# Queries, keys and all gates as units of seven products, one root for all norms, heads between the products

## The chip, the cores and the metric

The kernel runs on one core of a Trainium2 chip. The core has a matrix engine (TensorE, "PE" in the profile; its weight loads are "PEld"), a vector engine (VectorE, DVE), a scalar engine (ScalarE, ACT), GpSimd (POOL) and SyncE (SP), which issues every DMA of this kernel. Each engine runs its own instructions in order, and semaphores order the engines among one another. The metric is the device time of one execution in microseconds (us); for a kernel the median of its runs is given. Everything is computed in float32.

## The reference

One decoder block over 1024 tokens of width 1024. What matters here is the first half: one input projection of the normalised input, whose columns are cut into attention queries, keys and values (12 heads of 128), retention q and k (4 heads of 256), retention v and its gate (2048 each) and two merge gates (1024 each).

```python
xn = rmsnorm(x, norm1_g[l])
qa, ka, va, qr, kr, vr, gr, gate_a, gate_b = [xn @ wl[:, bounds[i]:bounds[i + 1]] ...]
qa = rmsnorm(qa.reshape(B, S, ATT_HEADS, ATT_HEAD_DIM), q_norm_g[l])
ka = rmsnorm(ka.reshape(B, S, ATT_HEADS, ATT_HEAD_DIM), k_norm_g[l])
...
s = einsum(q, k) * (Dh ** -0.5) + bias          # ALiBi, causal window, dilated by 1, 4 or 16
p = exp(s - m);  den = sum(p);  o = (p @ v) / den;  lse = m + log(den)
o_a = sum over the three groups of softmax(lse) * o
o_r = head_groupnorm(retention(qr, kr, vr)) * silu(gr)
y = sigmoid(gate_a) * (o_a @ w_proj_a) + sigmoid(gate_b) * (o_r @ w_proj_b)
```

Then follow an output projection with a residual and a squared-ReLU MLP with another.

## The kernel before, in words

**Products.** A float32 operand is split into a high and a low part, `xh` and `xl` (line 318, `split`: ScalarE rounds the high part, L319, VectorE subtracts, L320). A product is the sum of three matmuls, high by high, high by low, low by high (`Pipe.group`, L218 to L230; the matmul is L223). TensorE's order is written out by hand: `Pipe.step` (L232) issues one product, and small tasks that were put down with `pipe.at(lag, fn)` are issued between the terms of the step `lag` steps later. The instructions of the other engines are ordered by a planner from its own estimate of times, the earlier in the program the more urgent; at run time every queue keeps that fixed order.

**Weights.** `Weights` (L38 to L204) loads pieces of weight from DRAM into raw buffers, splits them into six pairs of buffers, and lets the next piece in as a product frees its own. `add` takes a plain piece, `add_units` (L95) those of a unit of seven products.

**Units of seven products.** A block of 256 output columns by 1024 tokens is made of seven half-size products in place of eight (N1 to N7, `product`, L369 to L405, order in `strassen_order`, L257). A unit is 7 x 12 = 84 matmuls of 512 columns. Four of the seven operands are sums and differences of quarters of the input and lie ready in on-chip memory; the weight side's sums are made by VectorE (L121). As products end, ScalarE copies some PSUM banks (L388, L393, L396) and `result` gets the four quarters of the output.

**Order of the first half.**

1. Norm of the input, tile by tile (L548), turned by TensorE (L415) into the operands `X`.
2. Twelve heads (L564 to L679). For each of eight tiles of 128 tokens one step of 24 matmuls with 384 columns makes q, k and v together (L645). ScalarE squares q and k (L650), VectorE and GpSimd make the root of two sums (`rsqrt`, L330 to L333: GpSimd's power of -0.5), VectorE scales (L654), TensorE turns q and k (L660) into `qT` and `kT`. `attend` (L575) makes, for each of eight blocks, three tasks: scores (L584, with the maximum on VectorE at L587 and Exp on ScalarE at L591), the turn of the weights (L597, copied by VectorE at L599) and the product with the values (L604, copied by ScalarE at L606). They lie between the matmuls of later steps. Their PSUM tiles come from the pool `ms` of three. A head's result of 130 columns goes to `acc_d` in one to two DMAs (L612 to L618). Dilated heads send their values through DRAM (`v_d`) to gather them by stride.
3. Three gate blocks as plain products (L695 to L732), while the last head's attention ends; VectorE makes the sums and differences of the input (`differences`, L708).
4. 21 units (L767): five gates, eight of retention q and k, eight of the retention gate. `gate_out` (L687) takes a Sigmoid (L689); the retention gate takes another (L746); results go to DRAM.
5. Retention (L806 on), with the last head slot's mixing of the three groups (`load_heads`, `combine`: L432 to L478), and then the projections and the MLP, which the change leaves alone.

Of the kernel before, what the change touches and what calls it, by code (L numbers as in the profile page):

```python
# [10 lines left out]
F = mybir.dt.float32  # L11
# [6 lines left out]
P = 128  # L18
# [19 lines left out]
class Weights:  # L38
# [56 lines left out]
    def add_units(self, tag, srcs):  # L95
# [28 lines left out]
        for j in range(-1, len(srcs)):  # L124
            if j + 1 < len(srcs):
                r = base + 2 * (j + 1)
                piece((tag, j + 1, "A"), self.A[(j + 1) % 2], r + 1, both)
            if j >= 0:
                r = base + 2 * j
                piece((tag, j, "D"), (self.D, j % 2), r, slice(0, 512), lambda r=r: sums(r))  # L130
                piece((tag, j, "B"), self.B[j % 2], r + 1, both, lambda r=r: self.used.add(r + 1))
                piece((tag, j, "C"), self.C, r, both, lambda r=r: self.used.add(r))
        m = len(srcs)
# [136 lines left out]
def hybrid_block(ctx: ExitStack, tc: tile.TileContext, a: dict, out: bass.AP):  # L270
# [9 lines left out]
    big = pool(ctx, "big", 4)  # L280
# [14 lines left out]
    v_d = dram.tile([HEADS, S, DH], F, name="v_d")  # L295
# [9 lines left out]
    XS = {(j, i): slot_of(big) for i in range(2) for j in range(2)}  # L305
# [22 lines left out]
    const.tile([P, 224], F, name="rest")  # L328
# [89 lines left out]
    def dilated(g, b, src, dst):  # L418

        if g == 0:  # L420
            return src, dst[:, b * P:(b + 1) * P]
        r = 4 if g == 1 else 8
        src = src.rearrange("p (i r) -> p r i", r=r)
        if g == 1:
            nb, j = divmod(b, 4)
            return src, dst.rearrange("p (r i) -> p r i", r=r)[:, :, nb * P + 32 * j:nb * P + 32 * j + 32]
        return src, dst.rearrange("p (r i) -> p r i", r=r)[:, :, 16 * b:16 * b + 16]
# [4 lines left out]
    def load_heads(s, i, p2b):  # L432
        at = p2b.tile([P, 4, 3, DH + 2], F, name="at", bufs=1)
        rows = acc_d[512 * i:512 * i + 512].rearrange("(t p) (g s) e -> s p t g e", p=P, s=SLOTS)
        for t in range(4):
            tc.keep_in_program_order(nc.sync.dma_start(at[:, t], rows[s, :, t]))
        return at

    def combine(s, i, p2b, at):


        st = {}
        return [lambda: weigh(p2b, at, st), *(lambda t=t: mix(t, at, st) for t in range(4)),
                lambda: turn_mixed(s, i, p2b, st)]

    def weigh(p2b, at, st):
        w = st["w"] = p2b.tile([P, 6, 4], F, name="w")
        st["o"] = p2b.tile([P, 4, DH], F, name="oa")
# [23 lines left out]
    def turn_mixed(s, i, p2b, st):  # L472
        pt = tr.tile([P, 4, P], F, name="tr")
        for t in range(4):
            nc.tensor.transpose(pt[:, t, :], st["o"][:, t, :], ident)
        ot = p2b.tile([P, 512], F, name="oaT")
        nc.scalar.activation(ot, pt.rearrange("p t q -> p (t q)"), AF.Copy)
        nc.sync.dma_start(oa_d[s, :, 512 * i:512 * i + 512], ot)  # L478
# [11 lines left out]
    attn = ExitStack()  # L490
    p3 = pool(attn, "p3", 2, "right")
    p2 = pool(attn, "p2", 2, "right")
    cpa = pool(attn, "cpa", 1, "right")
    with ExitStack() as ph:
        cp = pool(ph, "cp", 1)
        first = ExitStack()
        px = pool(first, "px", 2)
        cmb = None

        g1 = cp.tile([P, D], F, name="g1")  # L500
        gq = cpa.tile([P, HEADS], F, name="gq")
        gk = cpa.tile([P, HEADS], F, name="gk")
        dist = cp.tile([P, 2, 2 * P], F, name="dist")
        row = px.tile([P, D], F, name="xn", bufs=3)
        ones = cp.tile([1, P], F, name="ones")
        xts = {}

        def load_x(t):
            xts[t] = px.tile([P, D], F, name="xt", bufs=3)
            nc.sync.dma_start(xts[t], a["x"][t * P:(t + 1) * P, :])  # L510

        xts[0] = px.tile([P, D], F, name="xt", bufs=3)
        for cs in halves():
            nc.sync.dma_start(xts[0][:, cs], a["x"][0:P, cs])
        nc.sync.dma_start(row[0:1, :], a["norm1_g"][None, :])
        nc.sync.dma_start(ident, a["c_ident"])
        W.load()
        W.load()
        load_x(1)
        W.load()  # L520
        ss = px.tile([P, 4], F, name="ss")
        xn = px.tile([P, D], F, name="xn", bufs=3)
        lo, hi = halves()
        gp = [mm.tile([P, 512], F, name="mm") for _ in range(2)]
        with tc.manual_schedule(engines={mybir.EngineType.DVE, mybir.EngineType.Activation}):
            nc.vector.memset(ones, 1.0)
            nc.scalar.activation(ss[:, 3:4], half[:, 0:1], AF.Square)
            for cs, pm in zip(halves(), gp):
                nc.tensor.matmul(pm, ones, row[0:1, cs], start=True, stop=True)
            nc.scalar.activation(xn[:, lo], xts[0][:, lo], AF.Square, accum_out=ss[:, 0:1])  # L530
            nc.vector.tensor_tensor_reduce(xn[:, hi], xts[0][:, hi], xts[0][:, hi], op0=OP.mult, op1=OP.add,
                                           scale=1.0, scalar=0.0, accum_out=ss[:, 1:2])
            nc.vector.tensor_tensor(ss[:, 0:1], ss[:, 0:1], ss[:, 1:2], op=OP.add)
            rsqrt(ss[:, 2:3], ss[:, 0:1], 1.0 / D)
            nc.vector.tensor_copy(g1[:, lo], gp[0])
            nc.vector.scalar_tensor_tensor(xn[:, lo], xts[0][:, lo], ss[:, 2:3], g1[:, lo], op0=OP.mult, op1=OP.mult)
            W.pump(1)
            nc.scalar.activation(g1[:, hi], gp[1], AF.Copy)
            nc.vector.scalar_tensor_tensor(xn[:, hi], xts[0][:, hi], ss[:, 2:3], g1[:, hi], op0=OP.mult, op1=OP.mult)
            put_transposed(xn, 0, 0)  # L540
            W.pump(1)
            put_transposed(xn, 0, 1)
            W.pump(1)
        load_x(2)
        load_x(3)
        W.pump(1)

        def norm1(t):  # L548
            if t not in xts:
                load_x(t)  # L550
            ss = px.tile([P, 4], F, name="ss")
            xn = px.tile([P, D], F, name="xn", bufs=3)
            nc.scalar.activation(xn, xts[t], AF.Square, accum_out=ss[:, 0:1])
            rsqrt(ss[:, 1:2], ss[:, 0:1], 1.0 / D)
            nc.vector.scalar_tensor_tensor(xn, xts[t], ss[:, 1:2], g1, op0=OP.mult, op1=OP.mult)
            pipe.at(t - 1 - pipe.slot, *[lambda q=q: put_transposed(xn, t, q) for q in range(2)])

        norm1(1)
        pipe.at(0, lambda: W.pump())
        nc.sync.dma_start(gq, a["q_norm_g"])  # L560
        nc.sync.dma_start(gk, a["k_norm_g"])
        nc.sync.dma_start(dist, a["c_dist"])

        for head, (slot, g) in enumerate(heads):  # L564
            h = g * SLOTS + slot
            slope = 2.0 ** (-8.0 * (h + 1) / HEADS)
            us = W.take(4)
            bias = p2.tile([P, 2 * P], F, name="bias")
            qT = p2.tile([P, S], F, name="qT")
            kT = p2.tile([P, S], F, name="kT")  # L570
            V = p2.tile([P, NT, DH], F, name="V")
            Vd = p2.tile([P, NT, DH], F, name="Vd") if g > 0 else V
            acc = p2.tile([P, NT, DH + 2], F, name="acc")

            def attend(g, h, b, bias, qT, kT, V, acc):  # L575

                nk = 2 if has_prev(g, b) else 1
                n = nk * P
                k0 = (b + 1 - nk) * P
                st = {}  # L580

                def scores():
                    sp = ms.tile([P, 512], F, name="ms")
                    nc.tensor.matmul(sp[:, :n], qT[:, b * P:(b + 1) * P], kT[:, k0:k0 + n], start=True, stop=True)  # L584
                    s = p3.tile([P, 2 * P], F, name="s")
                    mx = p3.tile([P, 1], F, name="mx")
                    nc.vector.tensor_tensor_reduce(s[:, :n], sp[:, :n], bias[:, 2 * P - n:], op0=OP.add, op1=OP.max,  # L587
                                                   scale=1.0, scalar=-3.0e38, accum_out=mx)
                    nc.vector.tensor_scalar(acc[:, b, DH:DH + 1], mx, -1.0, None, op0=OP.mult)
# [773 lines left out]
```

## Time and profile before

| what | value |
|---|---|
| time, median of 3 runs | 2261.97 us (2261.68 to 2267.01) |
| span of the profiled execution | 2267.2 us |
| its busy time on TensorE | 2233.0 us (98%) |
| VectorE / ScalarE / GpSimd busy | 57% / 45% / 15% |
| heads, 10.64 to 521.84 | 511.20 us |
| plain gates and the last head's end, to 595.36 | 73.52 us |
| 21 units, to 995.42 | 400.06 us |
| the rest, to the end | 1271.78 us |
| granted TensorE clock | 0.998 |

The profile is a trace of one execution; its span of 2267.2 us is that of the slowest of the three timed runs. Rows of instructions read: line, engine, operation, output <- inputs, shapes, count, then busy time, mean duration in ns of one, and the idle time of the engine before them. A row of one line's view has the duration as minimum/median/maximum, and the first and last start. A row of a timeline begins with start and duration in us. A row of stretches has the length, then the busy time and the instructions of each engine, the clock, the share of the DMA engines and GB/s. Matmuls overlap on TensorE, so that the mean duration of one (389 ns for 512 columns) is longer than the distance between two starts.

### The profile page before, as it was taken

The numbers are of one execution on the slowest core, as the hardware profiler recorded it, in microseconds if no ns is written. First come the engines' busy times: TensorE is split into PE (matmuls) and PEld (weight loads), VectorE is DVE, ScalarE is ACT, GpSimd is POOL, SyncE is SP. The second block draws the span as 40 slices with busy tenths as digits, with TensorE's granted clock in tenths as the row PEclk, the third lists the DMA queues.
The fourth block names the chain that finished last, engine by engine and source line by source line (L and its number), as shares of the span: only waits on it lengthen the run. The fifth ranks groups of instructions, "written<-read, shape, count | busy, mean of one in ns | idle before, by whom it ended". The sixth has DMA issues, their size and how long they took to land. (4 is left out here: it accounts for less than half of the span.)

```text
span 2267.2 us, 30458 instructions
## 1 busy us (share of the span) xinstructions
PE 2233.0 (98%) x10868; PEld 1912.0 (84%) x10868; DVE 1285.7 (57%) x2468; ACT 1014.0 (45%) x2294; POOL 344.3 (15%) x372
## 2 busy tenths in 40 slices
PE   8999999999999999999999999999999999899999
PEld 7999999998888888888888878888788888788777
DVE  6444545455544445558676753253855556687874
ACT  5444434345433333345555633112555545654542
POOL 1111111110000000000000000000000000587873
PEclk9999999999999999999999999999999999999999
DMA  4313232323233333363433385554345556645432
GB/s 148 98 52 105 65 91 85 94 85 99 82 109 106 110 109 111 113 186 117 122 117 97 121 267 183 155 184 153 107 127 151 151 152 199 218 153 179 169 129 102
DMA packets 227146, 294.85 MB, mean 130 GB/s; under 512 B 14129, under 2 KB 157873, under 8 KB 226994
## 3 DMA queue, kind: packets, MB, share of 16 engines
q1 hardware_dynamic: 226994, 292.91, 41.1%
q8 instruction: 85, 1.39, 0.3%
q14 instruction: 67, 0.55, 0.1%
HBM read 200.48 MB, written 92.37 MB: 129 GB/s over the span
## 5 line engine op out<-in xcount | busy, mean ns | idle before, releaser
L320 DVE TENSOR_TENSOR wl<-raw,wh 128x1024 fp32r<-128x1024 f32 (+2 forms) x274 | 300.4, 1099 | 398.0 <-ACT wh L319 396.9
L223 PE MATMUL mm<-wh,xh 128*128 128x384 f32 (+1 forms) x1226 | 482.0, 393 | 0.6 <-DVE Y L1203 0.5
L223 PE MATMUL mm<-wh,xl 128*128 128x384 f32 (+1 forms) x1226 | 438.8, 358 | 2.2 <-DVE xl L320 2.2
L223 PE MATMUL mm<-wl,xh 128*128 128x384 f32 (+1 forms) x1226 | 437.7, 357 | 0.0
L319 ACT ACTIVATE wh<-raw 128x1024 fp32r<-128x1024 f32 (+2 forms) x274 | 260.0, 951 | 358.2 <-PE ms L223 102.2
L223 PE MATMUL mm<-xl,wh 128*128 128x512 f32 x848 | 309.3, 389 | 1.7 <-DVE xl L320 1.7
L223 PE MATMUL mm<-xh,wh 128*128 128x512 f32 x848 | 309.7, 390 | 0.9 <-ACT ms L388 0.9
L223 PE MATMUL mm<-xh,wl 128*128 128x512 f32 x720 | 280.1, 389 | 0.0
L223 PEld LDWEIGHTS mm<-wh,xl 128*128 128x128 f32 x1226 | 230.9, 188 | 22.2 <-DVE xl L320 3.0
L223 PEld LDWEIGHTS mm<-wh,xh 128*128 128x128 f32 x1226 | 231.8, 189 | 20.0 <-DVE Y L1203 1.3
L223 PEld LDWEIGHTS mm<-wl,xh 128*128 128x128 f32 x1226 | 232.7, 190 | 16.6
L223 PE MATMUL ms<-xh,wh 128*128 128x512 f32 x604 | 239.3, 396 | 5.0 <-DVE s L941 3.5
L223 PE MATMUL ms<-xl,wh 128*128 128x512 f32 x604 | 235.8, 390 | 0.7 <-DVE xl L320 0.7
L223 PE MATMUL ms<-xh,wl 128*128 128x512 f32 x604 | 235.9, 391 | 0.0
L223 PEld LDWEIGHTS mm<-xl,wh 128*128 128x128 f32 x848 | 159.2, 188 | 34.9 <-DVE xl L320 2.1
L223 PEld LDWEIGHTS mm<-xh,wh 128*128 128x128 f32 x848 | 159.2, 188 | 34.2 <-ACT ms L388 1.3
L223 PEld LDWEIGHTS mm<-xh,wl 128*128 128x128 f32 x720 | 135.1, 188 | 28.1
L853 POOL TENSOR_TENSOR st<-st,half 128x1 f32<-128x1 f32 x32 | 25.8, 808 | 765.3 <-DVE st L852 765.3
L223 PEld LDWEIGHTS ms<-xh,wh 128*128 128x128 f32 x604 | 113.9, 189 | 31.2 <-issue 2.3
L223 PEld LDWEIGHTS ms<-xh,wl 128*128 128x128 f32 x604 | 113.7, 188 | 23.9
L223 PEld LDWEIGHTS ms<-xl,wh 128*128 128x128 f32 x604 | 113.9, 189 | 23.5 <-DVE xl L320 1.0
L333 POOL TENSOR_TENSOR ssa<-ssa,half 128x2 f32<-128x2 f32 x96 | 66.5, 693 | 427.9 <-DVE ssa L332 411.2
(296 smaller groups left out, 3605.1 us busy)
## 6 DMA issues: line engine op xcount, KB each, us to landing
raw<-in_w_att SPq DMA_DIRECT2D x48, 384.0 KB, 3.9
raw<-in_w_up SPq DMA_DIRECT2D x32, 512.0 KB, 3.9
h_d<-s SPq DMA_DIRECT2D x64, 256.0 KB, 4.5
raw<-in_w_down SPq DMA_DIRECT2D x32, 512.0 KB, 4.1
xh<-h_d SPq DMA_DIRECT2D x11, 896.0 KB, 4.5
xl<-h_d SPq DMA_DIRECT2D x10, 896.0 KB, 4.6
r<-h_d SPq DMA_DIRECT2D x10, 896.0 KB, 5.6
sg_d<-sg SPq DMA_DIRECT2D x32, 256.0 KB, 2.0
```

What stands on the lines that cost most here:

```text
L223: self.nc.tensor.matmul(ps, x, y, start=start, stop=stop, skip_group_check=not first)
L319: nc.scalar.activation(dst_h, src, AF.Copy)
L320: nc.vector.tensor_tensor(dst_l, src, dst_h.bitcast(F), op=OP.subtract)
L333: nc.gpsimd.tensor_tensor(dst, dst, half[:, :w], op=OP.pow)
L853: nc.gpsimd.tensor_tensor(st[:, 9:10], st[:, 8:9], half[:, 0:1], op=OP.pow)
```

## The change

Values come first: three plain blocks of 512 columns (four heads each, `w_av`), 8 tiles x 24 matmuls of 512 columns each, stored to `v_d`. The input's norm and `differences` lie between these steps. Then 36 units in one row: 12 for attention q and k (one head each), 8 for all gates, 8 for retention q and k, 8 for the retention gate. So the heads' 384-column products, the turns of q and k and the plain gates are gone.

For a head's unit, `result` copies the quarter on ScalarE with the tokens already put in order of the stride, stores it unnormalised to `qk_d`, squares it on ScalarE, splits the squares, and four slots later two matmuls with a column of ones (`pick`) add the 128 squares of each token into one row of a PSUM tile that holds all 48 rows (12 heads x q and k x two halves). After the last of them one power on GpSimd, 48 partitions by 512, makes all roots; they go to `rs_d`.

Heads then attend between the products of later units. Products are numbered from 0 to 251 in the order of the units (a slot). Head n begins at slot 103 + 12 n: three slots earlier `prepare` loads its q, k and the roots (broadcast over partitions), and VectorE multiplies q, k, root and gain in one instruction a half. Its eight blocks begin at slots 0, 1, 2, 3, 4, 6, 7, 8 of the twelve; scores come in the same slot, the turn two slots later, values four slots later, all three in PSUM tiles of the pool `tr` of two, the copy of the turned weights on ScalarE. Values come block by block from `v_d` (four buffers), a block's result goes to `acc_d` by a DMA of its own (`acc`, three buffers), and the mixing takes two tiles at a time. One of the operands, XS[0,1], is stored to DRAM (`xs_d`) before the units and loaded again for the retention, which makes the room. The biases are made on the host as constants in place of one instruction for each head.

```diff
-    for slot, g in heads:
+    for n in range(3):
         for u in range(4):
-            W.add(a["w_att"][g * SLOTS + slot, u])
-    for d, bufs in enumerate([(0, 1), (2, 4), (3, 5)]):
-        for u, b in enumerate(bufs):
-            W.add(a["w_gate"][d, u], b)
-    NG, NQ = KT - 3, 2 * RH
-    W.add_units("in", [a["w_gate_q"][j] for j in range(NG)] + [a["w_rqk_q"][j] for j in range(NQ)]
-                + [a["w_gr_q"][j] for j in range(8)])
+            W.add(a["w_av"][n, u])
+    NA, NG, NQ = HEADS, KT, 2 * RH
+    W.add_units("in", [a["w_aqk_q"][j] for j in range(NA)] + [a["w_gate_q"][j] for j in range(NG)]
+                + [a["w_rqk_q"][j] for j in range(NQ)] + [a["w_gr_q"][j] for j in range(8)], 1)
...
+        def square(n, f, i, sg):
+            x = sq.tile([P, 512], F, name="x", bufs=1)
+            hl = [sq.tile([P, 512], R, name=f"x{c}") for c in "hl"]
+            nc.scalar.activation(x, sg, AF.Square)
+            split(*hl, x)
+            m = 4 * n + 2 * f + i
+            def add():
...
+                for c, y in enumerate(hl):
+                    nc.tensor.matmul(to, pick[:, P - 1 - m:2 * P - 1 - m], y, start=sums["n"] + c == 0,
+                                     stop=sums["n"] + c == 8 * HEADS - 1)
+                sums["n"] += 2
+                if sums["n"] == 8 * HEADS:
+                    k = 4 * HEADS
...
+                    nc.vector.tensor_scalar(root[:k], to[:k], 1.0 / DH, EPS, op0=OP.mult, op1=OP.add)
+                    nc.gpsimd.tensor_tensor(root[:k], root[:k], power[:k], op=OP.pow)
+                    nc.sync.dma_start(rs_d, root[:k])
+            pipe.at(3, add)
...
+    FIRST, EACH, PAIR = 103, 12, 2
...
+                    raw = core.tile([P, 512], F, name="raw", bufs=2)
+                    rb = core.tile([P, 512], F, name="rb", bufs=2)
+                    nc.sync.dma_start(raw, qk_d[n, f, i])
+                    src = rs_d[4 * n + 2 * f + i]
+                    nc.sync.dma_start(rb, bass.AP(tensor=src.tensor, offset=src.offset, ap=[[0, P], [1, 512]]))
...
+            pipe.at(4, s3)
+            pipe.at(2, s2)
+            pipe.at(0, s1)
...
+        for n in range(HEADS):
+            p0 = FIRST + EACH * n
+            on(p0 - 3, lambda n=n: prepare(n))
+            for b in range(NT):
+                p = p0 + b * 6 // 5
+                on(p, lambda n=n, b=b: fetch(n, b))
+                on(p, lambda n=n, b=b: begin(n, b))
...
+        for p, (j, name) in enumerate(strassen_order(NIN)):
+            if p == FIRST - 4:
+                sqs.close()
+                plan_core()
+            for fn in events.pop(p, []):
+                fn()
             product("in", j, name, unit, operands, lambda: pu, result)
```

More of the change, by code (lines that the diff above doesn't have):

```diff
@@ L327, in hybrid_block @@
     gng = const.tile([P, 2, NF], F, name="gng")
-    const.tile([P, 224], F, name="rest")
+    gqk = const.tile([P, 2, HEADS], F, name="gqk")
+    const.tile([P, 200], F, name="rest")
     def rsqrt(dst, src, scale):
@@ L487, in mix_next @@
                 pipe.at(1, mixing.pop())
[L490 to L520, printed above, removed]
+    x01, gst, tst = ExitStack(), ExitStack(), ExitStack()
@@ new lines, in hybrid_block, with load_x @@
+    XS[0, 1] = slot_of(pool(x01, "x01", 1))
+    vp = pool(x01, "vp", 3)
+    first = ExitStack()
+    cp = pool(first, "cp", 1, "right")
+    px = pool(first, "px", 2, "right")
+    g1 = cp.tile([P, D], F, name="g1")
+    row = px.tile([P, D], F, name="xn", bufs=3)
+    ones = cp.tile([1, P], F, name="ones")
+    xts = {}
+    def load_x(t):
+        xts[t] = px.tile([P, D], F, name="xt", bufs=3)
+        nc.sync.dma_start(xts[t], a["x"][t * P:(t + 1) * P, :])
+    xts[0] = px.tile([P, D], F, name="xt", bufs=3)
@@ new lines, in hybrid_block @@
+    for cs in halves():
+        nc.sync.dma_start(xts[0][:, cs], a["x"][0:P, cs])
+    nc.sync.dma_start(row[0:1, :], a["norm1_g"][None, :])
+    nc.sync.dma_start(ident, a["c_ident"])
+    W.load()
+    W.load()
+    load_x(1)
+    W.load()
+    ss = px.tile([P, 4], F, name="ss")
+    xn = px.tile([P, D], F, name="xn", bufs=3)
+    lo, hi = halves()
+    gp = [mm.tile([P, 512], F, name="mm") for _ in range(2)]
+    with tc.manual_schedule(engines={mybir.EngineType.DVE, mybir.EngineType.Activation}):
+        nc.vector.memset(ones, 1.0)
+        nc.scalar.activation(ss[:, 3:4], half[:, 0:1], AF.Square)
+        for cs, pm in zip(halves(), gp):
+            nc.tensor.matmul(pm, ones, row[0:1, cs], start=True, stop=True)
+        nc.scalar.activation(xn[:, lo], xts[0][:, lo], AF.Square, accum_out=ss[:, 0:1])
+        nc.vector.tensor_tensor_reduce(xn[:, hi], xts[0][:, hi], xts[0][:, hi], op0=OP.mult, op1=OP.add,
+                                       scale=1.0, scalar=0.0, accum_out=ss[:, 1:2])
+        nc.vector.tensor_tensor(ss[:, 0:1], ss[:, 0:1], ss[:, 1:2], op=OP.add)
+        rsqrt(ss[:, 2:3], ss[:, 0:1], 1.0 / D)
+        nc.vector.tensor_copy(g1[:, lo], gp[0])
+        nc.vector.scalar_tensor_tensor(xn[:, lo], xts[0][:, lo], ss[:, 2:3], g1[:, lo], op0=OP.mult, op1=OP.mult)
+        W.pump(1)
+        nc.scalar.activation(g1[:, hi], gp[1], AF.Copy)
+        nc.vector.scalar_tensor_tensor(xn[:, hi], xts[0][:, hi], ss[:, 2:3], g1[:, hi], op0=OP.mult, op1=OP.mult)
+        put_transposed(xn, 0, 0)
+        W.pump(1)
+        put_transposed(xn, 0, 1)
+        W.pump(1)
@@ L521, in hybrid_block, with norm1 @@
+    load_x(2)
+    load_x(3)
+    W.pump(1)
+    def norm1(t):
+        if t not in xts:
+            load_x(t)
         ss = px.tile([P, 4], F, name="ss")
         xn = px.tile([P, D], F, name="xn", bufs=3)
[L523 to L556, printed above, removed]
@@ new lines, in norm1, with values @@
+        nc.scalar.activation(xn, xts[t], AF.Square, accum_out=ss[:, 0:1])
+        rsqrt(ss[:, 1:2], ss[:, 0:1], 1.0 / D)
+        nc.vector.scalar_tensor_tensor(xn, xts[t], ss[:, 1:2], g1, op0=OP.mult, op1=OP.mult)
+        pipe.at(t - 1 - pipe.slot, *[lambda q=q: put_transposed(xn, t, q) for q in range(2)])
+    def values(us, ts, last, from_=mm, name="mm"):
+        pm = from_.tile([P, 512], F, name=name)
+        terms = []
+        for k in range(KT):
+            wh, wl = W[us[k // 2]]
+            o = (k % 2) * 512
+            terms.append((*X(k, ts), wh[:, o:o + DV], wl[:, o:o + DV]))
+        ends = {2 * i + 1: (lambda i=i: W.free(us[i])) for i in range(4)} if last else None
+        pipe.step(pm, terms, ends)
+        return pm
@@ new lines, in differences @@
+    def differences(k):
+        x = {}
+        for j, i in ((0, 0), (0, 1), (1, 1), (1, 0)):
+            x[j, i] = xp.tile([P, 512], F, name=f"x{j}{i}")
+            xh, xl = XS[j, i]
+            nc.vector.tensor_tensor(x[j, i], xh[:, k].bitcast(F), xl[:, k].bitcast(F), op=OP.add)
+        for name, t, u, op in (("N5", (0, 0), (0, 1), OP.subtract), ("N7", (0, 1), (1, 1), OP.subtract),
+                               ("N6", (1, 1), (0, 0), OP.add), ("N4", (1, 0), (1, 1), OP.subtract)):
+            nc.vector.tensor_tensor(x[t], x[t], x[u], op=op)
+            split(operands[name][0][:, k], operands[name][1][:, k], x[t])
@@ new lines, in hybrid_block @@
+    norm1(1)
+    pipe.at(0, lambda: W.pump())
+    nc.sync.dma_start(gqk[:, 0], a["q_norm_g"])
+    nc.sync.dma_start(gqk[:, 1], a["k_norm_g"])
+    for n in range(3):
+        us = W.take(4)
+        for t in range(NT):
+            if n == 0 and t + 2 < NT:
+                norm1(t + 2)
+            if n == 0 and t == 2:
+                nc.vector.tensor_scalar(gqk[:, 0], gqk[:, 0], DH ** -0.5, None, op0=OP.mult)
+            if n == 1 and t == 0:
+                first.close()
+                ES = [slot_of(pool(gst, f"ext{i}", 1, "right")) for i in range(4)]
+                sgp = pool(gst, "sgp", 2, "right")
+                W.more = pool(gst, "more0", 1, "right")
+                xp = pool(tst, "xp", 1, "right")
+                operands = {"N1": XS[0, 0], "N2": XS[1, 0], "N3": XS[1, 1], "N5": ES[0], "N6": ES[1], "N7": ES[2],
+                            "N4": ES[3]}
+                for i, x in enumerate(XS[0, 1]):
+                    nc.sync.dma_start(xs_d[i], x.bitcast(F).rearrange("p a b -> p (a b)"))
+            if 8 * n + t in (9, 11, 13, 15):
+                differences((8 * n + t - 9) // 2)
+            ts = slice(t * P, (t + 1) * P)
+            pm = values(us, ts, t == NT - 1, ms, "ms")
+            vt = vp.tile([P, 512], F, name="vt")
+            nc.scalar.activation(vt, pm, AF.Copy)
+            nc.sync.dma_start(v_d[n, ts], vt)
@@ L682, in hybrid_block @@
+    assert not pipe.due
+    tst.close()
+    x01.close()
     nc.sync.dma_start(maskT, a["c_mask"])
@@ L733, in hybrid_block, with attend, scores, turn @@
-    assert attn is None and not todo
-    tst.close()
-    with ExitStack() as ph:
-        pu = pool(ph, "pu0", 2)
+    def attend(n, b, bias, qT, kT, V, core):
+        slot, g = heads[n]
+        h = g * SLOTS + slot
+        nk = 2 if has_prev(g, b) else 1
+        w = nk * P
+        k0 = (b + 1 - nk) * P
+        st = {}
+        acc = core.tile([P, DH + 2], F, name="acc", bufs=3)
+        def scores():
+            sp = tr.tile([P, 4, P], F, name="tr")[:, :nk].rearrange("p a b -> p (a b)")
+            nc.tensor.matmul(sp, qT[:, b * P:(b + 1) * P], kT[:, k0:k0 + w], start=True, stop=True)
+            s = st["p"] = core.tile([P, 2 * P], F, name="s", bufs=2)
+            mx = core.tile([P, 1], F, name="mx", bufs=2)
+            nc.vector.tensor_tensor_reduce(s[:, :w], sp, bias[:, 2 * P - w:], op0=OP.add, op1=OP.max,
+                                           scale=1.0, scalar=-3.0e38, accum_out=mx)
+            nc.vector.tensor_scalar(acc[:, DH:DH + 1], mx, -1.0, None, op0=OP.mult)
+            nc.scalar.activation(s[:, :w], s[:, :w], AF.Exp, bias=acc[:, DH:DH + 1], accum_out=acc[:, DH + 1:DH + 2])
+        def turn():
+            tp = tr.tile([P, 4, P], F, name="tr")
+            for j in range(nk):
+                nc.tensor.transpose(tp[:, j], st["p"][:, j * P:(j + 1) * P], ident)
+            st["t"] = core.tile([P, 2, P], F, name="pT", bufs=2)
+            nc.scalar.activation(st["t"][:, :nk], tp[:, :nk], AF.Copy)
+        def values():
+            po = tr.tile([P, 4, P], F, name="tr")[:, 0]
+            for j in range(nk):
+                nc.tensor.matmul(po, st["t"][:, j], V[b + 1 - nk + j], start=(j == 0), stop=(j == nk - 1))
+            nc.scalar.activation(acc[:, :DH], po, AF.Copy)
+            nc.sync.dma_start(tokens(acc_d[:, h, :], g, b), acc)
+        return scores, turn, values
@@ L738, in result @@
         def result(j, f, cs, src):
-            if j < NG:
-                gate_out(f, 3 + j, cs, src)
+            if NA <= j < NA + NG:
+                gate_out(f, j - NA, cs, src)
                 return
-            n = j - NG
+            if j < NA:
+                i = cs.start // 512
+                r = strides(heads[j][1])
+                sg = sgp.tile([P, 512], F, name="sg")
+                nc.scalar.activation(sg.rearrange("p (r i) -> p r i", r=r), src.rearrange("p (i r) -> p r i", r=r),
+                                     AF.Copy)
+                nc.sync.dma_start(qk_d[j, f, i], sg)
+                square(j, f, i, sg)
+                return
@@ L743, in result @@
+            n = j - NA - NG
             sg = src
@@ L1296, in _constants @@
     far = np.where((d >= 0) & (d <= P) & (k >= P) & (d % 2 == 0), d, BIG)
-    dist = np.stack([near, far], 1).astype(np.float32)
+    bias = []
+    for h in range(HEADS):
+        g = h // SLOTS
+        bias.append((near if g < 2 else far) * (-2.0 ** (-8.0 * (h + 1) / HEADS) * (DIL[g] if g < 2 else 8)))
     mask = np.zeros((P, RH, P), np.float64)
@@ L1323, in _layout @@
     gates = [np.concatenate([r(GA + d * P, P), r(GB + d * P, P)]) for d in range(KT)]
+    order = [g * SLOTS + slot for slot in range(SLOTS) for g in (1, 2, 0)]
     a = {
```

284 lines of the change are left out of this document (93 added, 191 removed).

## The prediction

> **What bounds the kernel now.** I read the page's busy times first, then four stretches of time, then what TensorE waits for.
>
> ```profile
> PE 2233.0 (98%) x10868; PEld 1912.0 (84%) x10868; DVE 1285.7 (57%) x2468; ACT 1014.0 (45%) x2294; POOL 344.3 (15%) x372
> ```
> ```profile
> core 0: us, PE busy (x) PEld busy (x) DVE busy (x) ACT busy (x) POOL busy (x), PEclk, DMA share, GB/s
> 10.64:521.84 511.20, 507.88 (x3137) 496.14 (x3136) 250.17 (x892) 235.58 (x927) 69.86 (x102) 1.00 0.29 88
> 521.84:595.36 73.52, 72.91 (x344) 59.77 (x343) 48.87 (x94) 35.33 (x69) 1.00 (x1) 1.00 0.26 87
> 595.36:995.42 400.06, 400.06 (x1765) 331.00 (x1764) 184.43 (x229) 147.50 (x212) 0.00 (x0) 1.00 0.34 112
> 995.42:1300.00 304.58, 303.93 (x1476) 252.03 (x1475) 221.74 (x506) 165.54 (x345) 24.21 (x29) 1.00 0.42 122
> ```
>
> The first stretch is the heads, the second the three plain gate blocks with the last head's attention, the third the 21 units of seven products, the fourth most of the retention. All the change lies before 995.42. TensorE is busy for all of 400.06 us in the units and for nearly all of the rest, so it is the bound, and time is won or lost as (matmul time) plus (new waits of TensorE). The retention row also says that a well-interleaved stage keeps TensorE full with VectorE at 73% and ScalarE at 54%.
>
> **The matmul time.** Matmuls overlap, so I price them from start to start. The unit row gives 400.06 / (21 x 84 = 1764) = 0.2268 us for 512 columns; a product of 12, one slot below, is 2.72 us. For 384 columns and for the pair of transposes:
>
> ```profile
> 59.51 0.34 PE L223 MATMUL mm<-wh,xl 128*128 128x384 f32 x1
> 59.69 0.38 PE L660 MATMUL tr<-ident,qk 128*128 128x128 f32 x2
> 59.82 0.42 PE L223 MATMUL mm<-wh,xh 128*128 128x384 f32 x1
> 60.08 0.33 PE L223 MATMUL mm<-wl,xh 128*128 128x384 f32 x1
> 60.26 0.34 PE L223 MATMUL mm<-wh,xl 128*128 128x384 f32 x1
> ...
> 63.90 0.34 PE L223 MATMUL mm<-wh,xl 128*128 128x384 f32 x1
> ```
> ```profile
> L223 PE MATMUL mm<-wh,xh 128*128 128x384 f32 x768 | 295.8, 385 | 0.0
> L223 PE MATMUL mm<-wh,xl 128*128 128x384 f32 x768 | 259.6, 338 | 2.2 <-DVE xl L320 2.2
> L223 PE MATMUL mm<-wl,xh 128*128 128x384 f32 x768 | 259.2, 338 | 0.0
> L660 PE MATMUL tr<-ident,qk 128*128 128x128 f32 x192 | 36.5, 271 | 0.0
> ```
>
> From 60.26 to 63.90 are 21 matmuls: 0.1733 us each. From 59.51 to 60.08 a pair of transposes stands between two of them: 0.57 - 2 x 0.1733 = 0.22 us a pair.
> Removed: 3 x 768 = 2304 x 0.1733 = 399.3; plain gates 3 x 4 x 24 = 288 x 0.2268 = 65.3; 96 pairs x 0.22 = 21.1. Together 485.7.
> Added: values 3 blocks x 8 tiles x 24 = 576 x 0.2268 = 130.6; 36 units in place of 21, 15 x 84 x 0.2268 = 285.8; sums of squares 96 x 0.2268 = 21.8. Together 438.2.
> Net -47.5 us. Scores, turns and value products of the heads stay as many as they were; only their place changes.
>
> **The root.** All 48 rows of sums (12 heads, q and k, two halves) now take one power on GpSimd, 48 partitions of 512 elements, in place of 96 of two elements.
>
> ```profile
> L333 POOL TENSOR_TENSOR ssa<-ssa,half x96: 688/689/996, 21.2 to 524.1; 128x2 f32<-128x2 f32 x96
> L333 POOL TENSOR_TENSOR ss<-ss,half x8: 545/547/1126, 5.6 to 38.4; 128x1 f32<-128x1 f32 x8
> L333 POOL TENSOR_TENSOR ssq<-ssq,half x8: 547/548/927, 1585.4 to 1635.1; 128x1 f32<-128x1 f32 x8
> ```
> ```profile
> L1170 POOL TENSOR_TENSOR xl<-xl,xh x43: 727/739/2899, 1939.0 to 2244.6; 128x256 fp32r<-128x256 f32 x43
> ```
>
> The medians are 547 ns for one element in a partition and 689 for two, both with a spread of a few ns over most of their executions: the second costs 142 ns. For 512 that makes 0.547 + 511 x 0.142 = 73.1 us. The other end is GpSimd's subtract, 739 ns for 256, so 1.5 us for 512. The two are far apart; I take 73, since its rows are the same operation on the same engine.
> [...]
>
> What waits for the root: the last square is added at the end of slot 91 of the units (unit 11's last product is slot 87, its square comes four later), and the first scores stand at the end of slot 103. Between lie 11.9 x 2.72 = 32.4 us. In that window must go the eviction of the sums, the power, the store to rs_d, and two rounds (two buffers) of load, then two products on VectorE.
>
> ```profile
> sg_d<-sg SPq DMA_DIRECT2D x32, 256.0 KB, 2.0
> s<-sg_d SPq DMA_DIRECT2D x32, 256.0 KB, 3.3
> acc_d<-acc SPq DMA_DIRECT2D x8, 260.0 KB, 3.3
> ```
> ```profile
> L1080 DVE SCALAR_TENSOR_TENSOR xn<-xr,ssq,g 128x512 f32<-128x512 f32 x8 | 6.0, 745 | 0.0
> ```
>
> 0.7 + 73.1 + (0.4 issue + 2.0) + 2 x (0.4 + 3.3 + 2 x 0.75) = 86.6 us. TensorE then stands for 86.6 - 32.4 = 54 us. The point from which it stands at all is a power of 19 us. The store of the root also blocks SP, which issues in order:
>
> ```profile
> SPq L176 <- DVE wl L320: 472.1, 122, 26.3
> ```
>
> Today's waits there reach 26.3 us at no cost. A wait of 73 us from slot 92 holds back the gates' stores, and with only two sg buffers ScalarE stops at the third gate result, about slot 94; the copy that the product of slot 98 adds to is then missing. TensorE would stop at slot 98 in place of 103, but the loads and products then run under the five slots that are left: 0.7 + 73.1 + 2.4 - 6 x 2.72 = 60 us. I keep 54 and put 60 in the range.
>
> **Heads between products.** Here TensorE's neighbours become tighter: three small tasks of a slot share two PSUM buffers (tr) where they had three (ms) and a step twice as long.
>
> ```profile
> L319 ACT ACTIVATE wh<-raw 128x1024 fp32r<-128x1024 f32 x181 | 191.4, 1058 | 297.5 <-PE ms L223 66.5 <-DMA raw<-in_w_up 56.3 <-PE mm L223 44.5
> L396 ACT ACTIVATE u<-ms 128x512 f32<-128x512 f32 x37 | 21.3, 576 | 0.0
> L591 ACT ACTIVATE pr<-s,acc 128x256 f32<-128x256 f32 x44 | 22.2, 505 | 47.9 <-DVE acc L589 40.7 <-PE tr L660 7.1
> L591 ACT ACTIVATE pr<-s,acc 128x128 f32<-128x128 f32 x52 | 20.9, 402 | 100.4 <-DVE acc L589 83.0 <-PE ms L584 8.1 <-PE mm L223 5.2
> L591 ACT ACTIVATION_READ_ACCUMULATOR pr<-s,acc 128x1 f32 x96 | 18.0, 187 | 0.0
> L606 ACT ACTIVATE acc<-ms 128x128 f32<-128x128 f32 x96 | 26.2, 273 | 27.5 <-PE ms L604 26.9
> ```
> ```profile
> L689 ACT ACTIVATE sg<-ms x17: 576/597/600, 530.2 to 700.1; 128x512 f32<-128x512 f32 x17
> L689 ACT ACT_TABLE_LOAD  x3: 1283/1283/1283, 528.9 to 546.5; - x3
> ```
> ```profile
> PE ms L597 <- ACT sg L689: 0.4, 1, 0.4
> PE ms L604 <- ACT sg L689: 0.2, 1, 0.2
> ```
>
> Sigmoid and Exp do not share a table: where gates met a head's end, each change cost a load of 1.283 us. Now the heads' Exps (slots 103 to 247) lie among the Sigmoids of the gates (to slot 143) and of the gr units (from about 195): some 90 slots, 60 blocks, 50 Sigmoids. In a unit with Sigmoids four neighbouring slots carry one each. There ScalarE has 4 x 0.60, a copy of 0.58, two weight pieces of 1.06, 2.7 blocks at 0.45 + 0.19 + 0.27 + about 0.3 (the pT copy moves here from VectorE), and about 5.3 loads: 15 us, in four slots of 2.72 + two thirds of a block (at most 1.0 us a block, since 511.20 + 73.52 - 485.7 leaves 99 us for 96), 13.3 us. Over the whole unit there is room. Upper end: 1.8 us in each of 13 units, 23. Lower end: 0.6 us over three Sigmoids as in the row above, 50 of them, 10. I take 15.
> The acc tile has three buffers and is held from scores to landed store, over four slots. A store of 66 KB lands in no more than the 3.3 us of the row for 260 KB, which brings the fourth and fifth block of a head to about their slot: 0 to 1 us for each of 24 blocks; I take 5.
>
> **Taken at nothing,** with the cover named. The squares' ScalarE and VectorE work lies under unit products where VectorE was busy 46% (third stretch). Value pieces of 1024 columns in place of 768 lie under value steps of 24 x 0.2268 = 5.4 us, which were 4.2; cover gone at the very start, they cost 1 us, and the two start-up waits (2.2 us in the 384 row above) may go. The copy of XS[0,1] to DRAM and back is needed only at the fifth retention step, some 25 us on; ahead of the first q and k loads on SP it could cost up to 5. VectorE's differences (48 operations) now lie under value steps. V loads have at least two slots, 5.4 us, against 3.3.
>
> **Sum.** The profiled execution has a span of 2267.2, as the slowest of the three runs (2267.01), and stands 5 us over their median: 2267.2 - 47.5 + 54 + 15 + 5 = 2293.7, +26.5. Against the median of 2262.0 that is 2288 us.
>
> **Rivals.**
> 1. The root is cheap, and the change is faster. The mechanism is the power's loop: if one more element of a long row costs under 35 ns, the power is done in 19 us and TensorE never stands. The time is then 2262 - 47.5 + 20 = 2234. For it: the subtract's 739 ns for 256, and that a loop of two need not show the pace of one of 512. Against it: 547 to 689 in the same operation. [...] Chance 0.22.
> 2. The power costs by partitions, 48 of 128: 73 x 48/128 = 27 us, and the wait is 8 us: 2242. With 60 ns an element it is 31 us and 2246; with 100 ns, 52 us and 2267. Chance 0.14.
> 3. The root is cheap, but the table loads become the bound. If every one of 60 blocks shows its two loads, 60 x 2.57 = 154 us; with a third of them on TensorE's path, 51, plus 5 for acc: 2262 - 47.5 + 56 = 2270. For it: two buffers of tr, which ScalarE has to empty within about 2 us, while one load with its Sigmoid is 1.9. Against it: only 0.6 us of TensorE's waits in the overlap of today. [...] Chance 0.12.
>
> **Numbers.** My forecast, a root that TensorE waits for some 54 us: 0.52, 2288, with its own range 2268 (short acc and table waits, 5 in all, and a power 10% cheaper) to 2316 (60 for the wait, 40 for the rest). Something under 0.3% (6.8 us) can't be told from no change in this kernel. Faster: rival 1 and some of rival 2, 0.27; same 0.06; slower: forecast, rival 3 and the rest, 0.67. The range 2234 to 2316 leaves out half of rival 1 and a tenth above.
>
> **What would show it.** One power of about 73 us on GpSimd; a gap of TensorE of 50 to 60 us shortly before the first scores, after which it stays full; stores on SP held back by GpSimd for as long; 36 x 84 unit matmuls at 0.227 us; no 384-column ones; 50 to 100 table loads of 1.283 us, with TensorE's waits on them in fractions of a us. A power under 20 us makes the forecast wrong by its whole sign; waits on ScalarE of over 2 us a unit would make it too low.

## The result and the profile after

The changed kernel takes 2355.19 us (median; 2352.79 to 2356.32) against 2263.02 us for the kernel before beside it: a ratio of 1.0405, 95% interval 1.0391 to 1.042. The direction was forecast, the size was not: 92 us more, where +26 was said, and outside the range.

The profiled execution has a span of 2351.0 us. First the page's busy times and three rows of its 40 slices (each digit is the busy share of a slice in tenths; in the row PEclk it is the granted clock):

```profile
PE 2208.5 (94%) x10016; PEld 1803.7 (77%) x10016; DVE 1325.6 (56%) x2364; ACT 1166.7 (50%) x2123; POOL 359.7 (15%) x277
...
PE   9999999419899999899999999999999999899999
...
POOL 0000000760000000000000000000000000478883
PEclk9999999759999999999999999999999999999999
```

TensorE is busy for less time than before (2208.5 against 2233.0 us), over a longer span. Its hole is in slices 8 and 9, and in these two GpSimd is busy, as it is again only in the last six. By stretches (start and end, length, then busy time and instructions of each engine, the clock third from the end): value blocks, units up to the power, the power and the gap, the rest of the units, and the rest of the kernel.

```profile
11.20:150.40 139.20, 139.11 (x634) 114.67 (x633) 65.70 (x95) 51.36 (x82) 4.22 (x7) 1.00 0.37 129
150.44:424.10 273.66, 273.66 (x1203) 225.44 (x1202) 140.94 (x184) 164.62 (x243) 0.00 (x0) 1.00 0.29 101
424.10:523.00 98.90, 21.45 (x84) 16.92 (x82) 9.53 (x12) 5.93 (x10) 82.19 (x1) 0.62 0.14 47
523.00:1085.50 562.50, 525.73 (x2495) 424.70 (x2496) 308.18 (x822) 350.84 (x707) 0.00 (x0) 0.98 0.53 166
1085.50:2351.00 1265.50, 1242.93 (x5594) 1019.34 (x5592) 795.85 (x1242) 587.99 (x1076) 272.52 (x264) 0.99 0.48 154
```

In the third stretch TensorE works for 21 of 99 us; in the fourth, where the heads lie between products, it is idle for 37 of 562. In the first two it is busy throughout, so values first, the squares and the units cost no wait. What TensorE waited for, longest first (engine and tile, what it waited for, us in total, times, longest):

```profile
PE ms L223 <- ACT u L394: 74.2, 1, 74.2
PE tr L645 <- ACT s L640: 22.7, 16, 3.5
PE tr L634 <- ACT acc L653: 7.8, 6, 2.8
...
PE mm L223 <- ACT ms L389: 4.5, 1, 4.5
...
PE tr L645 <- ACT pT L647: 3.0, 4, 1.4
```

L640 is the heads' Exp, L653 and L647 the copies of their value products and turned weights. The one long wait is for a copy of ScalarE (L394), which itself is short. What stands behind it is shown by three views: the groups of instructions, the waits of all engines and those of SP's queue.

```profile
L758 POOL TENSOR_TENSOR root<-root,power 48x512 f32<-48x512 f32 x1 | 82.2, 82187 | 384.1 <-DVE root L757 384.1
```
```profile
ACT sg L619 <- DMA sg_d<-sg: 84.7, 2, 82.0
...
DVE acc L639 <- DMA acc_d<-acc: 31.3, 24, 3.5
```
```profile
SPq L759 <- POOL root L758: 90.0, 1, 90.0
```

The power takes 82.2 us. SP stands at the store of the root for 90 us, with the gates' stores behind it in the queue; so ScalarE waits 82.0 us for one of two sg buffers; and TensorE waits for the copy that stands behind this on ScalarE's queue. The wait of 31.3 us is VectorE's, for the acc buffers of the heads. ScalarE's rows of table loads show one thing more: 17 for the gates' Sigmoids and 31 for the heads' Exp, and with those of the retention gate and of the mixing 73 in all, where there were 7:

```profile
L619 ACT ACT_TABLE_LOAD  x17: 1283/1283/1283, 386.9 to 688.4; - x17
```
```profile
L640 ACT ACT_TABLE_LOAD  x31: 1283/1283/1283, 538.7 to 1045.3; - x31
```

### The profile page after: what moved, and what is told of

It reads as the page before. It is cut to its first block, busy times and chain, and to the rows that moved or that the text cites. A ratio compares the mean times of both kernels' runs of the same rounds, so it can differ in the third digit from the quotient of the medians.

```text
span 2351.0 us, 28915 instructions
## 1 busy us (share of the span) xinstructions
PE 2208.5 (94%) x10016; PEld 1803.7 (77%) x10016; DVE 1325.6 (56%) x2364; ACT 1166.7 (50%) x2123; POOL 359.7 (15%) x277
## 5 line engine op out<-in xcount | busy, mean ns | idle before, releaser
L323 DVE TENSOR_TENSOR wl<-raw,wh 128x1024 fp32r<-128x1024 f32 (+1 forms) x292 | 327.8, 1124 | 364.9 <-ACT wh L322 360.4
L223 PE MATMUL mm<-xh,wh 128*128 128x512 f32 x1088 | 425.7, 410 | 4.9 <-ACT ms L389 4.5
L322 ACT ACTIVATE wh<-raw 128x1024 fp32r<-128x1024 f32 (+1 forms) x292 | 282.4, 969 | 280.9 <-PE ms L223 94.3
L223 PE MATMUL mm<-xh,wl 128*128 128x512 f32 x960 | 378.4, 394 | 0.0
L223 PE MATMUL ms<-xh,wh 128*128 128x512 f32 x688 | 283.7, 412 | 77.9 <-ACT u L394 74.2
L223 PE MATMUL mm<-wh,xh 128*128 128x512 f32 x458 | 186.3, 407 | 0.6 <-DVE Y L1236 0.4
L223 PE MATMUL mm<-wh,xl 128*128 128x512 f32 x458 | 179.4, 392 | 0.0
L223 PE MATMUL mm<-wl,xh 128*128 128x512 f32 x458 | 178.5, 390 | 0.0
L758 POOL TENSOR_TENSOR root<-root,power 48x512 f32<-48x512 f32 x1 | 82.2, 82187 | 384.1 <-DVE root L757 384.1
L223 PEld LDWEIGHTS mm<-wh,xl 128*128 128x128 f32 x458 | 85.9, 188 | 19.2
L223 PEld LDWEIGHTS mm<-wh,xh 128*128 128x128 f32 x458 | 86.2, 188 | 17.4 <-DVE Y L1236 1.3
L223 PEld LDWEIGHTS mm<-wl,xh 128*128 128x128 f32 x458 | 86.4, 189 | 15.6
```

What stands on the lines that cost most here:

```text
L223: self.nc.tensor.matmul(ps, x, y, start=start, stop=stop, skip_group_check=not first)
L322: nc.scalar.activation(dst_h, src, AF.Copy)
L323: nc.vector.tensor_tensor(dst_l, src, dst_h.bitcast(F), op=OP.subtract)
L758: nc.gpsimd.tensor_tensor(root[:k], root[:k], power[:k], op=OP.pow)
```

## The experiments

All kernels below are edits of the changed kernel, and ratios are to the kernel before, run beside them.

**Without the power.**

```diff
-nc.gpsimd.tensor_tensor(root[:k], root[:k], power[:k], op=OP.pow)
+nc.vector.tensor_tensor(root[:k], root[:k], power[:k], op=OP.mult)
```

> Leaves out the root's power (VectorE multiplies in its place, so the heads' norm is not that of the reference). Theory: the power of 82.2 us is what TensorE waits for, 74.2 us at the unit product that needs a copy of ScalarE and 4.5 us at the next, and some 3 us of half clock behind the gap, so 2355 - 82 = 2273 us, still slower than before, with the waits for Exp and the copies of the heads (about 38 us) left as they are. Rival: the first head's chain of loads and products would hold TensorE anyway, and a wait of over 20 us stays near the first scores: 2300 or more.

Measured: 2274.97 us, ratio 1.005 (1.0034 to 1.0067). This kernel leaves the root out. Neither the long wait nor the one of 4.5 us is among TensorE's nine longest, which go down to 1.4 us; its waits begin with those of the heads:

```profile
PE tr L645 <- ACT s L640: 24.0, 16, 4.1
PE tr L634 <- ACT acc L653: 9.1, 6, 2.8
```

So the root accounts for 80 us, and without it the change would still not be faster: the heads' waits stay.

**One table for Exp and the gates.** Sigmoid as a tanh of half the argument. The outer factor and the added one go into products that are there anyway (the merge gates' products, the residual of the output projection, the gain of the group norm).

```diff
-nc.scalar.activation(sg, src, AF.Sigmoid)
+nc.scalar.activation(sg, src, AF.Tanh, scale=0.5)
...
-nc.vector.tensor_tensor(sga, sga, pp, op=OP.mult)
+nc.vector.scalar_tensor_tensor(sga, sga, 1.0, pp, op0=OP.add, op1=OP.mult)
...
-nc.vector.tensor_tensor(y, pm, xt, op=OP.add)
+nc.vector.scalar_tensor_tensor(y, pm, 0.5, xt, op0=OP.mult, op1=OP.add)
```

> Every Sigmoid becomes a tanh of half the argument, with the rest folded into products that are there already; Exp and tanh are expected to share one table, so the 73 table loads go to a handful. Theory, the loads make the Exps late: TensorE's waits for Exp (22.7 us) and for the heads' copies (7.8 + 3.0) fall below 8 in all, with some half clock behind the longest of them, 2355 - 30 = 2325 us. Rival, the three acc buffers make them late: the waits stay above 20 us and the time within 8 us of 2355.

Measured: 2328.05 us, 27 us less than the change. The number of table loads is shown for a later kernel, the last of the three with a cheap root below: tanh and one square root more, and ScalarE runs 2054 instructions there where the change runs 2123. With the square root counted, 70 of the 73 loads are gone, so the 96 Exps and the tanhs among them hardly ever need a load in between. The waits for copies went from 7.8 and 3.0 to 1.6 us together; those for Exp only from 22.7 to 14.7:

```profile
PE tr L646 <- ACT s L641: 14.7, 13, 3.2
...
PE tr L653 <- ACT pT L648: 1.4, 1, 1.4
...
PE tr L635 <- ACT acc L654: 0.2, 1, 0.2
```

The time is as the theory said, but the waits are not: 16 us of them are left where under 8 were expected. So something else makes Exps late as well.

**Five acc buffers.**

```diff
-acc = core.tile([P, DH + 2], F, name="acc", bufs=3)
+acc = core.tile([P, DH + 2], F, name="acc", bufs=5)
```

> Five acc buffers in place of three, nothing else. Rival of the table loads, the acc buffers make the Exps late: waits for Exp fall from 22.7 to under 8 us, 2355 - 20 = 2335 us. Theory of the table loads: the waits stay at 15 us or more, 2345 to 2357 us. If both count, each alone gives a part.

Measured: 2329.46 us, 26 us less than the change. The waits for Exp are gone from TensorE's list altogether; those for the copies of ScalarE have grown from 7.8 to 13.7:

```profile
PE tr L634 <- ACT acc L653: 13.7, 10, 2.6
...
PE tr L645 <- ACT pT L647: 1.7, 2, 1.4
```

So both count. The late Exps come from the acc buffers first: VectorE writes the maximum into acc before Exp can start, and in the change it waited for a store to land 24 times, 31.3 us in all, unevenly spread over ten of the twelve heads. The late copies come from the table loads.

**The law of the power.** Five more powers, results unused, ahead of the units.

```diff
+for m, w in ((P, 8), (P, 64), (48, 64), (P, 256), (16, 256)):
+    nc.gpsimd.tensor_tensor(pa[:m, :w], pa[:m, :w], pb[:m, :w], op=OP.pow)
```

> Five more powers on GpSimd while it is idle ahead of the units: 128x8, 128x64, 48x64, 128x256 and 16x256, results unused. Theory, the cost goes by elements in a partition whatever the number of partitions: about 0.4 us + 0.142 to 0.160 us an element, so 1.5 to 1.7, 10, 10, 37 to 41 and 37 to 41 us, the time unchanged within 0.3% of 2355. Rival, it goes by partitions too: 48x64 takes some 3/8 of 128x64, and 16x256 an eighth of 128x256.

Measured, in the groups of GpSimd:

```profile
L618 POOL TENSOR_TENSOR probe_a<-probe_a,probe_b 128x256 f32<-128x256 f32 x1 | 41.2, 41237 | 0.1
L618 POOL TENSOR_TENSOR probe_a<-probe_a,probe_b 16x256 f32<-16x256 f32 x1 | 41.2, 41216 | 0.1
...
L618 POOL TENSOR_TENSOR probe_a<-probe_a,probe_b 128x64 f32<-128x64 f32 x1 | 10.6, 10557 | 0.1
L618 POOL TENSOR_TENSOR probe_a<-probe_a,probe_b 48x64 f32<-48x64 f32 x1 | 10.5, 10538 | 0.1
...
L618 POOL TENSOR_TENSOR probe_a<-probe_a,probe_b 128x8 f32<-128x8 f32 x1 | 1.6, 1648 | 109.0 <-DVE probe_b L616 109.0
```

Partitions do not matter (16 against 128: 41.216 and 41.237 us). An element of a partition costs (41237 - 10557) / 192 = 160 ns, and 512 of them 10.56 + 448 x 0.160 = 82.1 us, which is the change's 82.2. The time did not stay: 2462.12 us (one run), 107 more. TensorE now also waited 102.3 us on ScalarE's copy at L389. The probe's pool is closed before that of the squares is opened. The author's reading is that the squares' tiles got its room, and that VectorE's first write of one of them (`pick`) stood behind the powers, 105 us in all; no view here shows that wait. The prices hold; of the time, the expectation was wrong.

**A cheap root, then the other two repairs on top.** The root as ScalarE's square root and VectorE's reciprocal on the same tile.

```diff
-nc.gpsimd.tensor_tensor(root[:k], root[:k], power[:k], op=OP.pow)
+nc.scalar.activation(root[:k], root[:k], AF.Sqrt)
+nc.vector.reciprocal(root[:k], root[:k])
```

> The same change with the root by ScalarE's square root and VectorE's reciprocal on the same 48 x 512 tile, nothing else. Theory: both together take a few us, under the 19 us from which TensorE waits, so the wait of 74 us and that of 4.5 us go and the time is that of the run without the power, 2275 us (2268 to 2282). Rival, the head's first chain of loads holds TensorE anyway: over 2290.

> Square root and reciprocal, and five acc buffers. Theory: the waits for Exp (24 us in the run without the power) go as they did with the power in place, 2275 - 26 = 2249 us, faster than before by 0.6%. Rival, that the acc buffers gain only in what the long gap left behind: 2265 or more.

> Square root and reciprocal, five acc buffers, and tanh in place of Sigmoid. Theory: no wait of the heads over 1 us is left and no half clock behind them; table loads take the waits for ScalarE's copies (13.7 us with five buffers) with them: 2249 - 14 = 2235 us. If the two causes were one and the same wait, it stays at 2245 to 2250.

Measured: 2273.76 us with the root alone, ratio 1.0036 (1.0023 to 1.0048); 2250.23 with five acc buffers, 0.9935 (0.992 to 0.995); 2227.46 with tanh as well, 0.9835 (0.982 to 0.9849). The square root took 0.63 us behind one table load of 1.28, the reciprocal 3.34. The last of the three is faster than both kernels, by 1.65% than the kernel before the change. Its time is 8 us better than expected, since tanh gave 23 us here and not 14. Its busy times, and the longest of what TensorE waits for at its heads' tasks and at the unit products:

```profile
PE 2192.8 (98%) x10016; PEld 1796.4 (81%) x10016; DVE 1330.3 (60%) x2366; ACT 1076.9 (48%) x2054; POOL 277.4 (12%) x276
```
```profile
PE tr L646 <- ACT pT L648: 2.2, 2, 1.3
...
PE tr L635 <- DVE w L454: 0.8, 1, 0.8
...
PE ms L223 <- ACT u L397: 0.6, 1, 0.6
```

**Where TensorE stops.** The store of the root from GpSimd's queue, in place of SP's.

```diff
-nc.sync.dma_start(rs_d, root[:k])
+nc.gpsimd.dma_start(rs_d, root[:k])
```

> The power stays; only the store of the root is issued by GpSimd, so that SP does not stand behind the power from slot 92. Theory, as the prediction's second reading: TensorE stops at slot 98 because the gates' stores stand behind the root's store; without that SP stands only at the first load of the roots (from slot 100), TensorE stops later, at the third gate result behind it or at the first scores, and the gap is 82.2 + 13.5 - 32.4 = 63 us in place of 74 + 4.5, the time some 12 us less, 2343. Rival, the planner already puts the loads of the roots ahead of the gates' stores: no change, 2355.

Measured: 2352.07 us (one run), no change. SP stands at the next instruction that needs the root, a load of it, for 79.4 us, and TensorE for 78.9 us one product later than before:

```profile
SPq L682 <- DMA rs_d<-root: 79.4, 1, 79.4
```
```profile
ACT wh L322 <- DMA raw<-in_w_gate_q: 94.8, 6, 84.7
...
DVE qT L684 <- DMA rb<-rs_d: 78.9, 1, 78.9
```
```profile
PE mm L223 <- ACT ms L389: 78.9, 1, 78.9
```

The rival was right: the planner had put that load early too. What ScalarE lacks is another thing than in the change, though: no wait for an sg buffer is among the longest of all engines, which go down to 11.0 us, but it waits 84.7 us for the next piece of weight, whose load stands behind that of the root on SP's queue. Taking one instruction off the queue does nothing here, since another one with the same wait stands there. VectorE stands as well, at its first product with a root (L684), 78.9 us here and 80.1 in the change. No run frees SP's queue or VectorE's alone, so whether VectorE by itself would stop TensorE is not shown.

**A shorter power.** The first w columns by GpSimd, the rest by VectorE, with w = 256 and then 128; the kernels leave out the root of the rest.

```diff
+nc.vector.tensor_tensor(root[:k, w:], root[:k, w:], power[:k, w:], op=OP.mult)
-nc.gpsimd.tensor_tensor(root[:k], root[:k], power[:k], op=OP.pow)
+nc.gpsimd.tensor_tensor(root[:k, :w], root[:k, :w], power[:k, :w], op=OP.pow)
```

> The power takes 256 of the 512 columns (41.2 us by the probe); VectorE multiplies the rest, so half the tokens' norm is not the reference's. Theory, SP stands behind the root's store and TensorE stops at slot 98, some 16 us after the power begins: the gap shortens by the 41 us saved, from 74.4 + 4.7 to about 34 + 4, the time is 2355 - 41 = 2314 us.

> The power takes 128 columns (20.7 us), VectorE the rest, which leaves out three quarters of the norm. Theory, TensorE stops at slot 98 behind SP: the gap is 74.4 - 61.5 = 13 us, perhaps with the 4 us behind it, 2274 + 13 to 17 = 2287 to 2291 us. Rival, the prediction's first reading, TensorE waits only at the first scores, from a power of 19 us on: a gap of 2 us, 2276 us.

Measured: 2315.51 us with 256 columns, the power 41.5 us; 2293.84 with 128, the power 21.2. TensorE's waits for the copy, of the first and then of the second:

```profile
PE ms L223 <- ACT u L394: 33.5, 1, 33.5
```
```profile
PE ms L223 <- ACT u L394: 13.4, 1, 13.4
```

From 82.2 to 41.5 to 21.2 us the gap goes 74.2, 33.5, 13.4: each microsecond of power is one of gap, and the line meets zero at a power of about 8 us. The wait at the next product stays at 4.5 to 5.1 us. The first reading of the prediction, a wait only at the first scores and only from 19 us on, would have left about 2 us of the last; it falls.

**The power alone.** Five acc buffers and tanh, with the power of the change.

> The power as in the change, five acc buffers and tanh: only the root's wait is left. Theory, the three causes add: 2227.5 + 79 + some 3 us of half clock behind the gap = 2310 us, and the heads' waits on ScalarE are below 5 us in all. Rival, the waits of the heads and the gap share time: 2320 or more.

Measured: 2307.42 us, ratio 1.0198 (1.0181 to 1.0215). The gap is 74.1 us, and no wait for an Exp is among TensorE's seven longest, which go down to 1.8 us. Against the same kernel with the cheap root, 2227.46, the root costs 80 us; against the change, 2355.19, the two repairs gain 48 us with the power in place and 46 without it (2273.76 to 2227.46). The causes add.

## Why the prediction was wrong in size

**The matmul time** was about right: -47.5 us was said. The kernel with all three repairs stands 38.1 us under the kernel before beside it (2227.46 against 2265.59) with hardly a wait left in the first half, so some 9 us of that gain did not show. TensorE's busy time fell by 40.2 us (2233.0 to 2192.8), so most of what is missing lies in the price of matmuls and not in waits; of which ones, no run here tells.

**The root, 54 us taken: the mechanism was right, two terms of its sum were too small.** The price of an element was taken from one and two elements, 142 ns; over long rows it is 160, and the power is 82.2 us in place of 73.1. And of the two readings of who waits first, the prediction took the scores at slot 103 and kept the other for its range. The runs show the other: SP's queue stands behind the store, the third Sigmoid finds no sg buffer, and TensorE stops after 98 products of the units. The reading's sum of 60 us becomes 69 with the measured power; measured are 74.2, and 4.5 at the next product while loads that had queued behind the root land. The rest lies behind the power: TensorE starts again 8.3 us after its end (506.3 to 514.6), where the sum has 2.4, for the sg stores have to land first, and then two Sigmoids, a split of weights and the copy follow one another on ScalarE. As a whole the root costs 80 us.

**The heads between products, 15 and 5 us taken, 46 to 48 measured.** The table loads were priced at 10 to 23 us and gave 23 to 27; the upper end was the better one. The acc buffers are the term that failed most: 0 to 1 us for each of 24 blocks, the fourth and fifth of each head, 5 taken. The trace shows 24 waits of VectorE for a store to land, 31.3 us, 1.3 us each and up to 3.5. That the number agrees is luck: they lie in ten of the heads on the fourth to eighth blocks, only 12 of them on the fourth and fifth. The stores land in 2.3 us in the median but in up to 6.3, where 3.3 was taken as the most. Five buffers gave 24 to 26 us. A block whose Exp is late holds TensorE at its turn two products on. Together, 26 us of the root, 26 to 28 of the heads and some 9 of the matmuls make up most of the 66 us by which the forecast rise was too small. The range, by its own terms, is 2266 to 2314 us in place of 2268 to 2316, which decides nothing here.

**Not in the sum at all: the clock.** Behind the long gap TensorE ran its first 11 matmuls at a granted clock of 0.50 (0.43 us from start to start in place of 0.23), and behind the wait of 4.5 us it ran so again for 6.8 us. Where the heads lie between products there are three more such stretches, of 6.8, 3.4 and 3.4 us, each at a wait: 2.8, 2.5 and 3.5 us. The stretch behind the wait of 4.5 us, with the granted clock third from the end:

```profile
522.70:529.50 6.80, 5.17 (x12) 4.11 (x13) 3.62 (x4) 3.63 (x5) 0.00 (x0) 0.50 0.61 173
```

By the spans between starts, matmuls took about 10 us longer in these five stretches than at full clock. These are part of the 80 us of the root and of the 46 to 48 of the heads, and not a cause beside them.

**The rivals.** The cheap root (rival 1, 2234 us) is not what happened, and its own time was too good by 40 us: with the root free the change took 2274, mostly since its 20 us for the heads were too few. Rival 2, the cost by partitions, is refuted by the probe. Rival 3 took the root to be cheap, which it was not. For the kernel with the cheap root it names the right place and nearly the time (2270 said, 2274 measured), in part by luck: it has 51 us of loads and 5 of acc where the loads gave 23 to 27 and acc 24 to 26, and its total of 56 us, too large by 8 to 10, makes good the gain of the matmuls that did not show.

## What to carry to other kernels

An operation that is cheap on one or two elements should be priced by its slope before many are merged into it, and the slope measured on a long row. A long wait need not be paid where its result is used: here it was paid at the instructions that stood behind the store of the root in SP's queue (90.0 us). Follow each queue that stands to the buffers that it frees and the loads that it still has to issue. When tasks are laid between shorter products, each buffer's hold time (from first write to landed store) over the distance of two tasks gives an estimate of the buffers needed; three were too few here and five enough, and four were not tried. A table shared by the functions that now alternate was worth about as much here as the two more buffers (23 to 27 us and 24 to 26).

## What was not expected of the hardware

GpSimd's power cost 160 ns for each element in a partition, with few partitions as with many: 41.2 us for 16 x 256 as for 128 x 256. The same engine subtracted 128 x 256 in 0.74 us (the median in the kernel before). VectorE's reciprocal of 48 x 512 took 3.34 us and ScalarE's square root 0.63 us with a table load of 1.28 us, 5.3 us together in place of 82.2.
